# Output and down projections of a decoder trunk: two column chunks together, seven products on sums in place of eight for 42 channel pairs

## The chip, the cores and the metric

The kernel runs on one core of a Trainium2 chip. The metric is the device time of one execution in microseconds (us). Engines are named as the profile names them: PE is the matrix engine (PEld its weight loads), DVE the vector engine, ACT the scalar engine, POOL the GpSimd engine, SP the engine that issues most DMAs. An instruction queue is worked off in order on each engine; engines wait for one another by semaphores.

## The reference

A hidden state of 256 tokens by 2048 channels passes through one Mamba-2 layer with a gated feed-forward network (FFN) and one attention layer with a second FFN; after each of the four parts comes `x <- LayerNorm(alpha * x + f(x))`. What matters here are three matrix products:

```python
y @ w_out                                # 256 x 4096 by 4096 x 2048, end of the Mamba mixer
(jax.nn.silu(gate) * val) @ w_down       # 256 x 5632 by 5632 x 2048, end of either FFN
h = layer_norm(DEEPNORM_ALPHA * h + mix, ln_mix_g[layer], ln_mix_b[layer])
```

All is float32. The kernel splits each float32 operand into a high part, rounded to the type that PE multiplies fast, and a low part (the rest), and computes high*high + high*low + low*high: three matmuls for one product.

## The kernel before, in words

**Weights.** The matrices lie in DRAM cut into tiles of 128 x 1024 float32 (512 KB), in the order of use. One tile is one *step*. `load()` (L165) fetches a tile into one of four `raw` buffers, with a DMA on SP's queue. `split()` (L175) makes the high part `hi` on ACT (a cast, L191) and the low part `lo` on DVE (a subtraction, L192), in a ring of four buffers each, and then issues the next load. `splits(i)` (L196) is called once in step i and lets the splits run at most three steps ahead of the products.

**Output and down projections (mode "X").** The 2048 output columns are four chunks of 512. A chunk is the sum over all channels: `w_out` has 32 channel tiles of 128, `w_down` 44. A step holds two channel tiles (a *channel pair*) of one chunk. `half(i, t)` (L204) makes the products of 128 tokens (t is 0 or 1) with the step's two 128 x 512 weight blocks: six matmuls, so twelve in a step. The activations are stationary: `yT` (after the Mamba mixer) or `gT` (in an FFN) hold high and low parts with channels on partitions. Chunk after chunk is finished; the last four steps of the fourth chunk (eight at the kernel's end) are its *tail*, whose second token half comes at the very end in two pieces of 256 columns. The other big products (mode "W") put the weights in the stationary place.

**PSUM.** Eight banks of 128 x 512: three pairs `acc` and two single tiles `tp`.

**Norm.** `class Norm` (L373 on) adds each finished chunk to alpha times the residual (`add2`, `begin`, `add`), gathers statistics, and normalises; `chain` (L863 on) hangs these onto steps: `at(i, f)` runs f after the products of step i, `amid` in their middle, `beyond` after one half. `turn` transposes the result into `hT`, the input of the next products.

**Where the activations come from.** Mamba: for each of eight groups of 512 channels (16 steps and some small products each) `z_split(g)` (L817) writes the high and low part of 512 channels into `yT`, 12 steps into the following group. FFN: `gated(j, half)` (L974) does so for 256 channels into `gT`. During the three projections `hT` (128 x 16 channel tiles x high and low x 256 tokens) is not read, apart from serving as extra split buffers in the last steps.

**Order.** There is no scheduler: each engine gets its instructions in the order in which the Python code runs.

## Time and profile before

| | |
|---|---|
| median of three runs | 2517.62 us (2517.26 to 2519.15) |
| profiled execution, its own time | 2518.55 us |
| its span, first to last instruction | 2516.6 us |
| PE busy in the span | 2502.3 us (99%) |
| DVE, ACT, POOL busy | 1664.1, 1366.1, 75.8 us |
| bytes moved by DMA | 503 MB, 200 GB/s |
| mean granted TensorE clock | 0.999 |

The three projections lie at about 490 to 670 us (Mamba), 1155 to 1395 us (first FFN) and 2263 to 2506 us (second FFN) of the span. Times below are microseconds from the span's start. A busy matmul in the profile lasts longer than its share of the stream, since matmuls overlap: what one costs is read from how many start in a stretch.

### The profile page before, as it was taken

What the parts mean: (1) busy time and instruction counts of PE and PEld (TensorE: products, weight loads), DVE (VectorE), ACT (ScalarE), POOL (GpSimd) and SP (SyncE); (2) the same over time, 40 slices, a digit from 0 to 9 for tenths busy, and PEclk for the clock granted to TensorE, in tenths of its full rate; (3) what the DMA queues carried; (4) which work ended last, traced back from release to release, by engine and by line L of the source; (5) the groups of instructions that cost most, each with busy time, mean ns of one, the idle gap of its engine ahead of it and who ended that gap; (6) DMA issues with size and microseconds to landing.
All of it is one profiled execution on the core that took longest, in us unless ns stands there. A gap on an engine that the chain in (4) does not pass through costs nothing.

```text
span 2516.6 us, 35530 instructions
## 1 busy us (share of the span) xinstructions
PE 2502.3 (99%) x13711; PEld 2159.3 (86%) x13711; DVE 1664.1 (66%) x2134; ACT 1366.1 (54%) x1779; POOL 75.8 (3%) x96
## 2 busy tenths in 40 slices
PE   9999999999999999999999999999999999999998
PEld 8888888888888888888888888888888888888887
DVE  7878778855766767675445656655776776775545
ACT  6677787643465555554334445543555555554333
POOL 0000000000200000000000200000200000000001
PEclk9999999999999999999999999999999999999999
DMA  7665665666666565656676665457666566566575
GB/s 265 201 191 193 216 200 181 205 206 221 212 210 197 188 195 189 197 186 197 202 237 208 212 193 169 160 173 236 211 200 196 189 195 190 193 193 202 197 226 167
DMA packets 142264, 503.07 MB, mean 200 GB/s; under 512 B 15872, under 2 KB 16384, under 8 KB 142096
## 3 DMA queue, kind: packets, MB, share of 16 engines
q1 hardware_dynamic: 136976, 483.45, 58.9%
q0 software_dynamic: 4832, 16.85, 2.2%
q8 instruction: 107, 1.75, 0.3%
q14 instruction: 61, 0.50, 0.1%
q10 hardware_dynamic: 288, 0.52, 0.1%
HBM read 492.30 MB, written 8.45 MB: 199 GB/s over the span
## 4 chain that ended last, share of the span: by engine, by line
PE 96%; DVE 2%; DMA 1%; ACT 1%; issue 1%; SPq 0%; DVEq 0%; ACTq 0%
PE acc L252 40%; PE acc L254 20%; PE acc L222 11%; PE acc L217 11%; PE acc L218 11%; DVE lo L192 1%; DMA raw<-in_w 1%; PE acc L756 1%; ACT hi L191 0%; PE tp L765 0%; PE acc L739 0%; PE tp L1029 0%; DVE r L431 0%; PE tp L1063 0%; PE tp L217 0%
## 5 line engine op out<-in xcount | busy, mean ns | idle before, releaser
L192 DVE TENSOR_TENSOR lo<-raw,hi 128x1024 fp32r<-128x1024 f32 (+1 forms) x871 | 1064.4, 1226 | 709.4 <-ACT hi L191 704.9
L191 ACT CAST hi<-raw 128x1024 fp32r<-128x1024 f32 (+1 forms) x871 | 912.6, 1050 | 870.5 <-PE acc L222 396.0
L252 PE MATMUL acc<-hT,hi 128*128 128x512 f32 x4496 | 1083.8, 392 | 0.5 <-ACT hi L191 0.5
L252 PEld LDWEIGHTS acc<-hT,hi 128*128 128x128 f32 x4496 | 822.3, 188 | 160.0 <-ACT hi L191 1.0
L254 PEld LDWEIGHTS acc<-hT,lo 128*128 128x128 f32 x4496 | 556.1, 188 | 24.7 <-DVE lo L192 1.3
L254 PE MATMUL acc<-hT,lo 128*128 128x256 f32 x4496 | 563.3, 277 | 0.9 <-DVE lo L192 0.9
L218 PE MATMUL acc<-lo,gT 128*128 128x512 f32 x668 | 259.6, 389 | 0.0
L217 PE MATMUL acc<-hi,gT 128*128 128x512 f32 x668 | 259.6, 389 | 0.0
L222 PE MATMUL acc<-hi,gT 128*128 128x512 f32 x668 | 205.5, 389 | 0.0
L218 PEld LDWEIGHTS acc<-lo,gT 128*128 128x128 f32 x668 | 125.4, 188 | 26.0
L217 PEld LDWEIGHTS acc<-hi,gT 128*128 128x128 f32 x668 | 125.4, 188 | 25.9
L222 PEld LDWEIGHTS acc<-hi,gT 128*128 128x128 f32 x668 | 125.3, 188 | 26.0
L217 PE MATMUL acc<-hi,yT 128*128 128x512 f32 x244 | 95.0, 389 | 0.0
L218 PE MATMUL acc<-lo,yT 128*128 128x512 f32 x244 | 94.7, 388 | 0.0
L217 PE MATMUL acc<-hi,hT 128*128 128x512 f32 x192 | 78.8, 410 | 0.0
L566 DVE TENSOR_TENSOR u<-u,acc 128x512 f32<-128x512 f32 x108 | 73.5, 682 | 7.9 <-ACT u L565 7.9
L593 DVE SCALAR_TENSOR_TENSOR g<-u,cols,g 128x254 f32<-128x254 f32 (+1 forms) x176 | 73.5, 478 | 4.8 <-ACT g L588 4.8
L218 PE MATMUL acc<-lo,hT 128*128 128x512 f32 x192 | 75.4, 393 | 0.0
L222 PE MATMUL acc<-hi,yT 128*128 128x512 f32 x244 | 74.9, 388 | 0.0
L979 ACT CAST gT<-v 128x512 fp32r<-128x512 f32 x44 | 27.3, 621 | 84.6 <-DVE v L978 84.6
L593 DVE SCALAR_TENSOR_TENSOR v<-u,cols,v 128x254 f32<-128x254 f32 (+1 forms) x176 | 73.1, 477 | 0.0
L424 POOL TENSOR_TENSOR rs<-rs,mhalf 128x1 f32<-128x1 f32 x8 | 7.4, 930 | 1981.1 <-DVE nb L425 1981.1
(234 smaller groups left out, 1809.7 us busy)
## 6 DMA issues: line engine op xcount, KB each, us to landing
raw<-in_w SPq DMA_DIRECT2D x881, 512.0 KB, 4.0
mA<-acum_d POOLq DMA_DIRECT2D x16, 512.0 KB, 6.9
hres<-r POOLq DMA_DIRECT2D x12, 512.0 KB, 6.3
r<-hres SPq DMA_DIRECT2D x12, 512.0 KB, 5.0
eA<-acum_d POOLq DMA_DIRECT2D x16, 128.0 KB, 8.6
r<-in_x SPq DMA_DIRECT2D x4, 512.0 KB, 5.2
gb<-in_ln_mix_g SPq DMA_DIRECT2D x8, 256.0 KB, 5.4
gb<-in_ln_mix_b SPq DMA_DIRECT2D x8, 256.0 KB, 5.5
```

What stands on the lines that cost most here:

```text
L191: nc.scalar.copy(h[:, sl], t[:, sl])
L192: nc.vector.tensor_sub(l[:, sl], t[:, sl], h[:, sl].bitcast(F32))
L217: nc.tensor.matmul(a, th, h[:, kk, sl], start=k == first, stop=False)
L218: nc.tensor.matmul(a, th, l[:, kk, sl], start=False, stop=False)
L222: nc.tensor.matmul(a, ch.x.lo(k)[:, ts], h[:, kk, sl], start=False, stop=k == last)
L252: nc.tensor.matmul(banks[j], h[:, (kk * nj + j) * P:(kk * nj + j + 1) * P], ch.x.both(k), start=begins, stop=ends, skip_group_check=True)
L254: nc.tensor.matmul(banks[j][:, :S], l[:, a, n * P:(n + 1) * P], ch.x.hi(k), start=begins, stop=ends, skip_group_check=True)
L424: nc.gpsimd.tensor_tensor(self.rs[:, h, :], self.rs[:, h, :], mhalf[:, 0, :], op=OP.pow)
L566: nc.vector.tensor_add(dst, dst, p[:, :, :S])
L593: nc.vector.scalar_tensor_tensor(d, u[:, i % 2, :S - k], c1(self.at_w, w[n - 1 - k] + self.ia + i), d, op0=OP.mult, op1=OP.add)
L756: nc.tensor.matmul(ps[64 * q:64 * q + 64, c, j * P:(j + 1) * P], G[g]["xdt"][:, c, h * 64:(h + 1) * 64], G[g]["A", c][:, h, :], start=True ...
L979: nc.scalar.copy(h, v[:, sl])
```

## The change

Two chunks of columns, a and b, are now worked together (`Duo`), in two duos for each projection. In a step the letters mean: `a` or `b`, a plain step as before (one channel pair, one chunk, twelve matmuls); `A` and `B`, two steps that share one channel pair. A *sum pair* has four activation blocks (two channel tiles by two token halves) and four weight blocks (two channel tiles by two chunks), so eight block products. They are replaced by seven, of sums of activation blocks with sums of weight blocks: `A` makes two of them, `B` five, three matmuls each, 21 in place of 24. The seven results go to eight PSUM banks, all there are. 4 and 6 channel pairs of the two duos of `w_out` and 8 and 8 of each `w_down` are sum pairs, 42 in all; the other pairs stay plain. The order of steps is set by `duo()`: some plain steps, then mostly `A B a b` repeated, then the rest of the plain ones.

- The sums of weights are made by `split_sums` on DVE (y = ra + rb's second block, z = y + a block of ra, and y's next), with high and low parts, in two tiles that were free then (`mA` or `gb`). A's raw tile is kept until B is split, and two loads are issued together after that.
- The ring of `hi` and `lo` has five buffers in place of four.
- The sums of activations are made earlier, 22 times, by `make_sums`, called from `z_split` (six times) and `gated(j, 0)` (eight times for each FFN). They are written to DRAM from SP's queue (512 KB each) and fetched into `hT` from POOL's queue at the beginning of the projection (`fetch_sums`).
- The results are put together by `Norm.sums`, nine DVE operations of 512 columns after the last sum pair of each duo.
- The residual is fetched at the beginning of a duo, and `add2` of the third chunk comes with the first `b` step after the last `a` step (for `w_out` that is the beginning of the tail).

The core of the diff:

```diff
+RING = LA + 2
+SUMS = {DI: (4, 6), DFF: (8, 8)}
+KEEP = 3
...
-    out += some("X", "mamba_w_out", 0, 0, 4, DI // P) + ffn(0)
+    out += duos("mamba_w_out", 0, DI // P, TAIL) + ffn(0)
...
+def duo(nk, which, tail):
+
+    sums = [2 * m for m in range(SUMS[nk * P][which])]
+    rest = [p for p in range(nk // 2) if p not in sums]
+    a, b, keep = list(rest), list(rest), max(tail, TAIL)
+    lead = "aaa" if which else "abababab" if nk == DI // P else "abababa"
+    items = [(n, {"a": a, "b": b}[n].pop(0)) for n in lead]
+    for p in sums:
+        items += [("A", p), ("B", p)]
+        if len(a) > KEEP:
+            items.append(("a", a.pop(0)))
+        if len(b) > keep:
+            items.append(("b", b.pop(0)))
+    return items + [("a", p) for p in a] + [("b", p) for p in b]
...
+    def split_sums(i):
+
+        ra, rb = raw_t.pop(i - 1), raw_t.pop(i)
+        (yh, yl), (zh, zl) = (ring_tiles() for _ in range(2))
...
+        nc.scalar.copy(wh, rb[:, 0])
+        yf, zf = (steps[i][0].tmp() for _ in range(2))
+        nc.vector.tensor_add(yf, ra, rb[:, 1:2, :].to_broadcast([P, 2, NC]))
+        nc.vector.tensor_sub(wl, rb[:, 0], wh.bitcast(F32))
+        nc.scalar.copy(yh, yf)
+        nc.vector.tensor_add(zf[:, 0], yf[:, 0], ra[:, 1])
+        nc.vector.tensor_add(zf[:, 1], zf[:, 0], rb[:, 0])
+        nc.vector.tensor_sub(yl, yf, yh.bitcast(F32))
+        nc.scalar.copy(zh, zf)
+        nc.vector.tensor_sub(zl, zf, zh.bitcast(F32))
+        hi_t[i], lo_t[i] = [wh, yh, zh], [wl, yl, zl]
+        load()
+        load()
...
+    def one(i, b, unit, h, l):
...
+        nc.tensor.matmul(a, xh, h, start=begins, stop=False)
+        nc.tensor.matmul(a, xh, l, start=False, stop=False)
+        nc.tensor.matmul(a, xl, h, start=False, stop=ends)
...
+        if name == "A":
+            one(i, "P1", (0, 0), h[:, 0], l[:, 0])
+            one(i, "p3", 3, h[:, 1], l[:, 1])
...
+        if name == "B":
+            (wh, yh, zh), (wl, yl, zl) = h, l
+            one(i, "P2", (1, 0), wh, wl)
+            one(i, "p5", 0, yh[:, 0], yl[:, 0])
+            one(i, "P7", 2, yh[:, 1], yl[:, 1])
+            run(mid, i)
+            one(i, "p6", 1, zh[:, 0], zl[:, 0])
+            one(i, "p4", (1, 1), zh[:, 1], zl[:, 1])
...
+    def make_sums(m, tile, v):
+
+        hi, lo = (tile.rearrange("p (a q t) -> p a q t", a=2, q=4)[:, a] for a in range(2))
+        (a11, a21), (a12, a22) = ([v[:, k, h * P:(h + 1) * P] for h in range(2)] for k in range(2))
+        nc.vector.tensor_sub(lo[:, 0], a21, a22)
+        nc.vector.tensor_sub(lo[:, 2], a11, a21)
+        nc.vector.tensor_sub(lo[:, 1], a11, lo[:, 0])
+        nc.vector.tensor_sub(lo[:, 3], a12, lo[:, 1])
+        nc.scalar.copy(hi.bitcast(F32R), lo)
+        nc.vector.tensor_sub(lo.bitcast(F32R), lo, hi)
+        nc.sync.dma_start(sums_d[m], tile)
+
+    def fetch_sums(m):
+        nc.gpsimd.dma_start(hT[:, 2 * m:2 * m + 2].rearrange("p k a t -> p (k a t)"), sums_d[m])
...
+            before(du.first - 2 + m // 3, fetch_sums, m)
...
+                at(du.sum_at[-1] + n, norm.sums, d, n)
...
+        if g < max(SUMS[DI]):
+            make_sums(g, mp.tile([P, 2 * NC], F32, tag="st", name="st", bufs=1), y[:, :2])
```

Where the change moves instructions: three places on DVE, the order before and now. L192 of before is L315 now, L821 is L1076, L723 is L973, L566 is L816, L416 and L419 (the third chunk's addition and statistics) are L631 and L658, L411 is L631.

First, DVE in the Mamba stage where the group's `z_split` stands (`mA` is the masked decay, `sz` the gate, `lo` a weight tile's low part). Before:

```order
L192 TENSOR_TENSOR lo<-raw,hi 128x2x512
L821 TENSOR_TENSOR yT<-y,yT 128x4x256
L723 TENSOR_TENSOR mA<-mA,cb 128x1024
L566 TENSOR_TENSOR sz<-sz,acc 128x512
L192 TENSOR_TENSOR lo<-raw,hi 128x2x512
```

Now, for six of the eight groups (`st` holds the sums of activations):

```order
L1076 TENSOR_TENSOR yT_160<-y_3929,yT_160 128x4x256
L570 TENSOR_TENSOR st_4374<-y_3929 128x128
L571 TENSOR_TENSOR st_4374<-y_3929 128x128
L572 TENSOR_TENSOR st_4374<-y_3929,st_4374 128x128
L573 TENSOR_TENSOR st_4374<-y_3929,st_4374 128x128
L575 TENSOR_TENSOR st_4374<-st_4374 128x512
L973 TENSOR_TENSOR mA_4099<-mA_4099,cb_4231 128x1024
L816 TENSOR_TENSOR sz_4383<-sz_4383,acc_4233 128x512
L315 TENSOR_TENSOR lo_4393<-raw_4270,hi_4392 128x2x512
```

Five operations stand between the low part of `yT` and the next mask; the last of them needs a cast of ACT that needs the four before it.

Second, DVE in the middle of the output projection. Before, one subtraction for each step and the addition of a finished chunk:

```order
L192 TENSOR_TENSOR lo<-raw,hi 128x1024 x16
L416 SCALAR_TENSOR_TENSOR r_5411<-r_5411,acc 128x512 x2
L419 BN_STATS bnst<-r_5411 128x6 x4
```

Now, for one `A B a b` (`mA` is y or z, `u` the low part of B's first block; the three subtractions of the last row are those of a, b and the next A):

```order
L284 TENSOR_TENSOR mA<-raw 128x1024
L285 TENSOR_TENSOR u<-raw,u 128x512
L287 TENSOR_TENSOR mA<-mA,raw 128x512
L288 TENSOR_TENSOR mA<-mA,raw 128x512
L289 TENSOR_TENSOR lo<-mA,hi 128x1024
L291 TENSOR_TENSOR lo<-mA,hi 128x1024
L315 TENSOR_TENSOR lo<-raw,hi 128x1024 x3
```

For the same four steps DVE has nine operations in place of four.

Third, DVE at the end of the output projection. Before:

```order
L192 TENSOR_TENSOR hT<-raw,hT 128x1024 x3
L192 TENSOR_TENSOR lo<-raw,hi 128x1024 x3
L411 SCALAR_TENSOR_TENSOR r_5997<-r_5997,acc 128x512
L401 SCALAR_TENSOR_TENSOR r_5997<-r_5997,acc 128x512
```

Now (`r2` is the residual of the third chunk, `r3` of the fourth):

```order
L315 TENSOR_TENSOR lo_6249<-raw_6201,hi_6248 128x1024
L631 TENSOR_TENSOR r2_5730<-r2_5730,acc_5656 128x512 x2
L658 BN_STATS bnst_4984<-r2_5730 128x6 x4
L315 TENSOR_TENSOR lo_6275<-raw_6223,hi_6274 128x1024
L315 TENSOR_TENSOR lo_6281<-raw_6227,hi_6280 128x1024
L631 TENSOR_TENSOR r3_5767<-r3_5767,acc_5732 128x512
L315 TENSOR_TENSOR lo_6294<-raw_6246,hi_6293 128x1024
L631 TENSOR_TENSOR r3_5767<-r3_5767,acc_5733 128x512
```

The third chunk's addition and statistics had 16 subtractions between them and the fourth chunk's first addition, and now have two; one more subtraction comes before the fourth chunk's second addition.

## Rows read from the trace of the kernel before

**Rows 1.** The page: the span, and busy time and share of each engine with its number of instructions.

```profile
span 2516.6 us, 35530 instructions
PE 2502.3 (99%) x13711; PEld 2159.3 (86%) x13711; DVE 1664.1 (66%) x2134; ACT 1366.1 (54%) x1779; POOL 75.8 (3%) x96
```

**Rows 2.** Who PE waited for over the whole run, the longest: us in total, times, longest.

```profile
PE tp L538 <- POOL ident masks.py:199: 1.4, 1, 1.4
PE acc L254 <- DVE lo L192: 0.9, 1, 0.9
```

**Rows 3.** Busy time of each engine (and its instructions) in stretches inside the three projections, then TensorE clock, busy share of the DMA engines and GB/s; the fourth stretch lies behind the end of the output projection, the last is the end of the span.

```profile
core 0: us, PE busy (x) PEld busy (x) DVE busy (x) ACT busy (x) POOL busy (x), PEclk, DMA share, GB/s
520.00:640.00 120.00, 120.00 (x531) 99.41 (x530) 65.65 (x71) 48.23 (x47) 0.00 (x0) 1.00 0.66 219
1200.00:1380.00 180.00, 180.00 (x795) 149.03 (x795) 89.91 (x86) 71.58 (x69) 0.00 (x0) 1.00 0.65 211
2300.00:2480.00 180.00, 180.00 (x796) 149.07 (x794) 88.66 (x85) 70.69 (x68) 0.00 (x0) 1.00 0.65 214
684.00:688.00 4.00, 3.78 (x20) 2.63 (x19) 4.00 (x6) 2.12 (x3) 0.53 (x1) 1.00 1.02 359
2510.00:2517.00 7.00, 0.00 (x0) 0.00 (x0) 2.35 (x5) 0.00 (x0) 2.27 (x2) 0.61 0.43 150
```

**Rows 4.** DVE in order of time, four places where its operations follow one another: start, us, line, tile, number of operations.

```profile
418.81 0.41 DVE L690 TENSOR_TENSOR cb<-tp,tri 128x256 f32<-128x256 f32 x1
419.14 1.22 DVE L192 TENSOR_TENSOR lo<-raw,hi 128x1024 fp32r<-128x1024 f32 x1
...
450.29 0.69 DVE L768 TENSOR_TENSOR eA<-eA,tp 128x512 f32<-128x512 f32 x1 [1.27 <-PE tp L765]
451.01 0.69 DVE L769 TENSOR_TENSOR y<-y,eA 128x512 f32<-128x512 f32 x1
...
478.42 0.42 DVE L809 SCALAR_TENSOR_TENSOR sz<-sz 128x256 f32<-128x256 f32 x1
478.88 0.42 DVE L810 SCALAR_TENSOR_TENSOR sz<-sz 128x256 f32<-128x256 f32 x1
...
680.15 2.30 DVE L192 TENSOR_TENSOR lo<-raw,hi 128x1024 fp32r<-128x1024 f32 x1
```

**Rows 5.** DVE in order of time around the sixth group's `z_split` (L821).

```profile
435.32 1.22 DVE L821 TENSOR_TENSOR yT<-y,yT 128x1024 fp32r<-128x1024 f32 x1
436.45 1.22 DVE L723 TENSOR_TENSOR mA<-mA,cb 128x1024 f32<-128x1024 f32 x1
437.59 0.68 DVE L566 TENSOR_TENSOR sz<-sz,acc 128x512 f32<-128x512 f32 x1
438.19 1.22 DVE L192 TENSOR_TENSOR lo<-raw,hi 128x1024 fp32r<-128x1024 f32 x1
439.32 1.28 DVE L741 TENSOR_TENSOR xdt<-acc,aux 128x512 f32<-128x512 f32 x2
440.52 0.68 DVE L742 TENSOR_TENSOR xe<-xdt,aux 128x512 f32<-128x512 f32 x1
441.12 3.49 DVE L192 TENSOR_TENSOR lo<-raw,hi 128x1024 fp32r<-128x1024 f32 x3
```

**Rows 6.** ACT's copy to `sz` there in order of time, the page's rows of ACT casts of 1024 and of 512 columns (count, then busy us and mean ns of one, then idle before), and PE in order of time there (L254 has the low parts of two steps, eight matmuls each).

```profile
434.12 0.58 ACT L565 COPY sz<-acc 128x512 f32<-128x512 f32 x1
...
L191 ACT CAST hi<-raw 128x1024 fp32r<-128x1024 f32 (+1 forms) x871 | 912.6, 1050 | 870.5 <-PE acc L222 396.0
L979 ACT CAST gT<-v 128x512 fp32r<-128x512 f32 x44 | 27.3, 621 | 84.6 <-DVE v L978 84.6
...
442.81 1.99 PE L254 MATMUL acc<-hT,lo 128*128 128x256 f32 x16
```

**Rows 7.** The first FFN, DVE behind `gated(j, 0)` and PE, in order of time.

```profile
1035.39 0.69 DVE L980 TENSOR_TENSOR gT<-v,gT 128x512 fp32r<-128x512 f32 x1 [0.69 <-ACT gT L979]
1036.54 1.23 DVE L192 TENSOR_TENSOR lo<-raw,hi 128x1024 fp32r<-128x1024 f32 x1 [0.45 <-ACT hi L191]
...
1042.49 1.99 PE L254 MATMUL acc<-hT,lo 128*128 128x256 f32 x16
```

**Rows 8.** Weight loads from issue to landing: the median between 520 and 640 us, and shortest, median and longest of the whole run.

```profile
raw<-in_w SPq DMA_DIRECT2D x44, 512.0 KB, 4.2
...
DMA to landing us min/median/max: 3.0/4.0/9.7
```

**Rows 9.** The beginning of the output projection: PE's first matmul and the addition on DVE that empties the last PSUM bank of the Mamba stage.

```profile
489.89 0.39 PE L217 MATMUL acc<-hi,yT 128*128 128x512 f32 x1
...
493.42 0.68 DVE L566 TENSOR_TENSOR sz<-sz,acc 128x512 f32<-128x512 f32 x1
```

**Rows 10.** The end of the output projection: DVE from the last two subtractions to the scaling of the first chunk, and the transposes (L357) on PE.

```profile
657.88 1.22 DVE L192 TENSOR_TENSOR lo<-raw,hi 128x1024 fp32r<-128x1024 f32 x1 [1.26 <-ACT hi L191]
659.95 1.23 DVE L192 TENSOR_TENSOR lo<-raw,hi 128x1024 fp32r<-128x1024 f32 x1 [0.84 <-ACT hi L191]
662.21 0.69 DVE L401 SCALAR_TENSOR_TENSOR r<-r,acc 128x512 f32<-128x512 f32 x1 [0.44 <-PE acc L222]
665.47 0.78 DVE L436 SCALAR_TENSOR_TENSOR r<-r,rs,gb 128x512 f32<-128x512 f32 x1 [0.47 <-POOL rs L424]
...
666.32 0.63 PE L357 MATMUL tp<-ident,r 128*128 128x128 f32 x4
```

More of the change, by code (lines that the diff above doesn't have):

```diff
@@ L193, in split, with in_ring @@
         hi_t[i], lo_t[i] = h, l
-        load()
+        if kind(i) != "A":
+            load()
+    def in_ring():
+        return sum(2 if kind(k) == "B" else 1 for k in hi_t if k not in spare)
     def splits(i, most=2):
@@ L200, in splits @@
             ahead = LA + 1 + sum(i <= k < j for k in spare)
-            if j < min(i + ahead, n_steps) and (j in spare or sum(k not in spare for k in hi_t) < LA + 1):
+            if j < min(i + ahead, n_steps) and (j in spare or in_ring() + (2 if kind(j) == "B" else 1) <= RING):
                 split()
@@ L208, in half @@
         sl = slice(0, NC) if piece is None else slice(piece * HC, (piece + 1) * HC)
-        a = ch.part[t] if piece is None else ch.piece[piece]
         ts = slice(t * P, (t + 1) * P)
-        cut_k = ch.nk - 2 * ch.tail
-        first = 0 if piece is None else cut_k
-        last = (cut_k if t and piece is None else ch.nk) - 1
-        for kk in range(2):
-            k = 2 * s + kk
+        if ch.mode == "D":
+            name, p = ch.items[s]
+            ks, side = (2 * p, 2 * p + 1), ch.sides[name]
+            if piece is None:
+                a, begins, ends = ch.into({"a": ("P2", "p4"), "b": ("p3", "N22")}[name][t], i)
+            else:
+                a, begins, ends = side.piece[piece], i == side.at[-side.tail], i == side.last
+        else:
+            ks, side = (2 * s, 2 * s + 1), ch
+            a = ch.part[t] if piece is None else ch.piece[piece]
+            cut_k = ch.nk - 2 * ch.tail
+            begins = ks[0] == (0 if piece is None else cut_k)
+            ends = ks[1] == (cut_k if t and piece is None else ch.nk) - 1
@@ L216, in half @@
+        for kk, k in enumerate(ks):
             th = ch.x.hi(k)[:, ts]
-            nc.tensor.matmul(a, th, h[:, kk, sl], start=k == first, stop=False)
+            nc.tensor.matmul(a, th, h[:, kk, sl], start=begins and kk == 0, stop=False)
             nc.tensor.matmul(a, th, l[:, kk, sl], start=False, stop=False)
         run(inner, (i, t, piece))
-        for kk in range(2):
-            k = 2 * s + kk
-            nc.tensor.matmul(a, ch.x.lo(k)[:, ts], h[:, kk, sl], start=False, stop=k == last)
+        for kk, k in enumerate(ks):
+            nc.tensor.matmul(a, ch.x.lo(k)[:, ts], h[:, kk, sl], start=False, stop=ends and kk == 1)
@@ new lines, in duo_products @@
+    def duo_products(i):
+        ch, s = steps[i]
+        ch.use(i)
+        name, p = ch.items[s]
+        h, l = hi_t[i], lo_t[i]
+        if name == "A":
+            one(i, "P1", (0, 0), h[:, 0], l[:, 0])
+            one(i, "p3", 3, h[:, 1], l[:, 1])
+            run(mid, i)
+            done(i)
+            return splits(i)
+        if name == "B":
[3 more added lines that the diff above has]
+            one(i, "P7", 2, yh[:, 1], yl[:, 1])
+            run(mid, i)
+            one(i, "p6", 1, zh[:, 0], zl[:, 0])
+            one(i, "p4", (1, 1), zh[:, 1], zl[:, 1])
+            done(i)
+            return splits(i)
+        side = ch.sides[name]
+        ends = side.tail and i >= side.at[-side.tail]
+        if side.tail and i == side.at[-side.tail]:
+            side.piece = [tp_tile()[:, :HC] if q or side.tail == LAST else acc_pair()[:, 0, :HC] for q in range(2)]
+        half(i, 0)
+        if ends:
+            if i < side.last:
+                return splits(i)
+            for q in range(2):
+                for j in side.at[-side.tail:]:
+                    half(j, 1, q)
+                    if q:
+                        done(j)
+            return
+        run(mid, i)
+        splits(i)
+        half(i, 1)
+        done(i)
@@ L980, in gated @@
             nc.vector.tensor_sub(lo, v[:, sl], h.bitcast(F32))
+            if half == 0 and j < max(SUMS[DFF]):
+                make_sums(j, t4k("st").rearrange("p a n -> p (a n)"), v[:, :2])
         for j, (cg, cv) in enumerate(up):
@@ L1096, in yoco_kernel @@
         spare[end - 3 + e] = 4 * e
-    at(down1[3].first + 6, n3.gb_psum, 0)
+    at(end - LAST + 1, n3.gb_psum, 0)
     at(end - LAST + 2, n3.gb_psum, 2)
@@ L1152 @@
         m = m if layer is None else m[layer]
+        if mode == "D":
+            for kind, p in duo(nk, *both):
+                tiles.append(_np.stack([m[k * P:(k + 1) * P, c:c + NC] for k, c in blocks(kind, p, c0)], axis=1))
+            continue
         for c, n, k, per in cut(mode, nk, both):
```

172 lines of the change are left out of this document (146 added, 26 removed).

## The prediction

> **What bounds the kernel now.** I read the page first: PE is busy 2502.3 of 2516.6 us, no other engine more than 66% [rows 1]. Then who PE waited for: no entry above 1.4 us, weights 0.9 us in all [rows 2]. Of the 14.3 us without PE, 7 or more lie behind its last matmul [rows 3]. So the time is the number of matmuls times their distance, and whatever feeds PE is hidden, with reserves that differ from place to place. [...]
>
> **The products.** 531, 795 and 796 matmuls start in 120, 180 and 180 us [rows 3]: 0.226 us each. Each of 42 channel pairs loses 24 - 21 = 3, together 126 x 0.226 = 28.5 us, all on the path. Everything below asks what of it is given back.
>
> **DVE inside the projections.** Operations of 1024 columns follow one another every 1.14 us (435.32, 436.45, 437.59), those of 512 every 0.60 (437.59 to 438.19) [rows 5], and one that needs the result of the one just before 0.72 (450.29 to 451.01) [rows 4]. Four steps needed 4 x 1.14 = 4.6 us of DVE beside 48 matmuls = 10.85 us. An `A B a b` needs six operations of 1024 (6.84) and three of 512 (0.60 + 0.60 + 0.72): 8.8 us beside 45 matmuls = 10.2 us. That is 86%, so PE still sets the pace, by 1.4 us a group. An addition with one operand repeated stands in no row. Its nearest row is the 1.14 above; the slowest subtraction of 1024 columns took 2.30 [rows 4], but at 680 us, beside POOL's elementwise work, and POOL computes nothing in the projections (busy 0.00 in them) [rows 3]. I take 1.14. With 2.30 for all six a group would take 15.7 us of DVE; that end goes into the last rival.
>
> **Weight loads.** A's and B's raw tiles come free together only when y and z are made, and two loads go out at once. That closes a loop: load L, cast of the next A on ACT (1.05 [rows 6] and some 0.05 to start), its subtraction (1.14), then y and z (1.14 + 0.60 + 0.60 + 0.72), less 0.66 because A's tile is free before the last addition: L + 4.7 us for one group. With the median landing of 4.2 us [rows 8] it is 8.9 us, under 10.2, so it is hidden. With L = 5.5 it equals PE's 10.2. Shortest and longest landing in the run are 3.0 and 9.7 [rows 8]. [...]
>
> **Making sums of activations, Mamba.** Here DVE has little reserve. Behind `z_split` it gets four subtractions of 128 columns and one of 512 that waits for ACT. A line through the distances 1.14, 0.60 and 0.33 (418.81 to 419.14) [rows 4, 5] gives 0.20 for 128 columns, and 0.33 where it needs the one before (0.46 instead of 0.33 for 256 columns, 478.42 to 478.88). From 436.45 the four end at 437.46; ACT, free from 434.12, casts 512 columns in 0.62 [rows 6], to 438.1; the last subtraction holds DVE until 438.74. Everything behind is 2.3 us later: the first of the three subtractions from 441.12 ends at 442.34 + 2.3 = 444.64. PE uses that low part in the second half of the sixteen matmuls from 442.81, at 443.72 [rows 6]. So PE waits 0.9 us where it had 1.4 us in hand. The other low parts have 3 us and more, and DVE catches up before the next group, so this comes once in each of six groups: 5.6 us. It is bounded by 0 (should DVE start this stretch earlier thanks to the fifth ring buffer) and 6 x 2.3 = 13.8 us.
>
> [...]
>
> **Making sums, FFN.** The same 2.3 us behind the low part at 1035.39 move the subtraction at 1036.54 to 1038.8; PE reads it in the block from 1042.49 [rows 7]. Nothing is lost. If that cover were gone, each of 16 calls could cost what a Mamba call does.
>
> **SP's queue.** Each store of sums waits on SP for DVE, with weight loads behind it. These loads wait for subtractions that stand behind the sums on DVE anyway, so SP adds nothing.
>
> **Fetching sums.** Six or eight fetches of 512 KB begin with each projection, beside weight loads that run the DMA engines at 65% and 211 to 219 GB/s; full, they moved 359 GB/s [rows 3]. The spare 140 GB/s moves 4 MB in 30 us. The first sums are needed after seven or eight steps of 12 x 0.226 = 2.7 us, 19 us and more, and one further pair every 10 us. If loads got only half of 359, a tile took 2.9 us to move instead of the 2.7 that PE needs: 1.7 us behind after eight steps. Bounds 0 and 1.7 for each projection; I take 0.5, since loads of up to 9.7 us cost PE almost nothing before [rows 2, 8]: 1.5 us in all.
>
> **Beginning and end of the output projection.** The second step now wants the bank that is emptied at 493.42 + 0.68 = 494.1; PE reaches the half that uses it at 489.89 + 18 x 0.226 = 493.96: 0.2 us waited [rows 9]. In the FFNs the bank's copy is not queued behind so much, 0. At the end, the third chunk's two additions and four statistics of 256 columns (2 x 0.60 + 4 x 0.33 = 2.5 us) and one more subtraction (1.14) come among operations that had 1.26, 0.84 and 0.44 us of idle time ahead of them [rows 10]. DVE is 3.6 - 2.5 = 1.1 us late at the addition of 662.21, hence at the scaling that the transposes of 666.32 need (665.47 + 0.78 = 666.25) [rows 10]: 1.0 us on PE. The FFNs have more steps between. Putting the seven results together takes nine operations, 6 us over three steps that leave 3 x (2.7 - 1.14) = 4.7; the rest runs into the next step, whose low parts are made three steps ahead.
>
> **The sum**, against the profiled execution's own 2518.55 us: -28.5 + 5.6 + 1.5 + 0.2 + 1.0 = -20.2, 2498.35 us. That execution stood 0.93 us above the median of the runs, so 2497.4 us.
>
> **Rivals.**
> - *The Mamba stage absorbs its share.* The fifth ring buffer lets ACT cast earlier, or DVE's backlog begins earlier. For it: DVE waited for ACT's casts in many places. Against it: in rows 5 DVE is busy without a gap, and order is fixed. All but about 1 us of the losses goes: 2490 us.
> - *The loop of loads sets the pace in part.* L at 5.7 us makes 10.4 a group, 0.2 x 42 = 8 us more: 2505 us. For it: two loads at once, the fetches beside them. Against: 4.2 us at 65% DMA.
> - *Slower: the same loop takes everything.* From L = 6.15 us on, an `A B a b` takes the 10.85 us of before, the 28.5 us are gone and the 8.3 us of losses stay: 2526 us. The place is the raw tiles of A and B; it decides from 6.15 us. DVE at 2 us for some of its six long operations (10.85 - 8.8 = 2.1 us more in a group) would do the same. For it: loads of up to 9.7 us. Against: that is over twice the median's excess over the shortest, in every group.
> - *The fetches stall the beginnings,* by the 1.7 us bound or somewhat more each time: 2502 us.
>
> **How the numbers follow.** Forecast 0.58, its own range 2493 to 2502; the first rival 0.17, the partial loop 0.12, the fetches 0.06, slower 0.07. The range 2488 to 2508 leaves out the slower case and the worse parts of the loop and fetches. A measurement of this kernel tells 0.2%, 5 us, from no change. Faster by that means below 2512.6: forecast, first rival, fetches and most of the loop, 0.89; within it 0.05 (a loop near break-even); slower 0.06.
>
> **What would show it.** 126 matmuls fewer, at 0.226 us. PE's waits: six of about 0.9 us on L315's low parts in the Mamba stage, at the first `lo` behind `xe`. In the projections DVE busy at 80 to 90% with gaps in each group and PE without; ACT waiting for raw tiles in the casts of A would be the loop's mark, PE waiting for L289 or L291 its price. Wrong would be: PE waits in every group, or waits for `hT` at the first A.

## The result and the profile after

The changed kernel takes 2504.69 us (median of four executions, 2503.27 to 2506.38) against 2517.57 us before: a ratio of 0.9948, 95% interval 0.9931 to 0.9965. It is faster by about 13 us. The forecast was 2497.4 us with a range of 2488 to 2508: the direction and the range hold, the middle is 7 us off. The profiled execution took 2503.27 us.

The page, as in [rows 1], and who PE waited for, as in [rows 2] (us in total, times, longest):

```profile
span 2501.6 us, 35870 instructions
PE 2477.3 (99%) x13585; PEld 2139.5 (86%) x13585; DVE 1898.3 (76%) x2509; ACT 1425.7 (57%) x1885; POOL 87.6 (4%) x118
```

```profile
PE tp L551 <- DVE r L675: 7.0, 3, 4.0
PE acc L447 <- DVE lo L315: 3.3, 6, 0.8
PE acc L352 <- DVE sz L816: 1.7, 1, 1.7
```

PE has 126 matmuls fewer, as reckoned, and three kinds of waits that it did not have. Where they lie is seen when the span is cut at the first matmul of each stage: stretch, its length, PE's busy time and matmuls, granted clock, DMA share, GB/s. The six stages are Mamba, output projection, first FFN up to its down projection, that projection, attention with the second FFN, last projection.

```profile
1.43:493.18 491.75, 488.31 (x3021) 1.00 0.65 215
493.18:672.35 179.17, 173.47 (x810) 0.99 0.67 228
672.35:1159.10 486.75, 486.60 (x2821) 1.00 0.60 206
1159.10:1392.83 233.73, 230.97 (x1038) 0.99 0.66 229
1392.83:2261.99 869.16, 868.40 (x4846) 1.00 0.59 200
2261.99:2491.22 229.23, 229.23 (x1057) 1.00 0.65 225
```

```profile
1.43:489.89 488.46, 487.08 (x3021) 1.00 0.64 207
489.89:668.23 178.34, 178.34 (x839) 1.00 0.65 218
668.23:1155.62 487.39, 487.09 (x2823) 1.00 0.60 195
1155.62:1395.75 240.13, 240.13 (x1085) 1.00 0.64 210
1395.75:2266.25 870.50, 869.54 (x4846) 1.00 0.59 194
2266.25:2506.12 239.87, 239.87 (x1104) 1.00 0.62 202
```

The second fence is the kernel before, cut in the same way. The differences of the lengths are +3.3, +0.8, -0.6, -6.4, -1.3 and -10.6 us, with -0.1 behind the last matmul: the 15.0 us by which the span is shorter. Products alone would give -6.8, -10.9 and -10.9 in the three projections (30, 48 and 48 matmuls of 0.2267, as 45 start in the 10.2 us of a group). The last projection has nearly its whole gain. The output projection gave all of its gain back and 0.8 more, the first down projection 4.5.

**The Mamba stage** shows the mechanism that was predicted. DVE behind the low part of `yT` in the third group, then PE at the low parts, in the first group and in the third (start, us, engine and line, operation, shape, count, idle time before and what ended it):

```profile
289.38 0.28 DVE L570 TENSOR_TENSOR st<-y 128x128 f32<-128x128 f32 x1
289.58 0.28 DVE L571 TENSOR_TENSOR st<-y 128x128 f32<-128x128 f32 x1
...
291.08 0.69 DVE L575 TENSOR_TENSOR st<-st 128x512 fp32r<-128x512 f32 x1 [0.69 <-ACT st L574]
291.69 1.22 DVE L973 TENSOR_TENSOR mA<-mA,cb 128x1024 f32<-128x1024 f32 x1
...
296.35 3.49 DVE L315 TENSOR_TENSOR lo<-raw,hi 128x1024 fp32r<-128x1024 f32 x3
```

```profile
198.26 1.22 PE L447 MATMUL acc<-hT,lo 128*128 128x256 f32 x8 [0.51 <-DVE lo L315]
...
296.04 1.08 PE L447 MATMUL acc<-hT,lo 128*128 128x256 f32 x8
297.63 1.22 PE L447 MATMUL acc<-hT,lo 128*128 128x256 f32 x8 [0.51 <-DVE lo L315]
```

The five operations hold DVE from 289.38 to 291.69, 2.31 us (predicted 2.3), and PE stands in the middle of the first `lo` behind `xe`, once in each of six groups. From one subtraction of `yT` to the next (L821 before, L1076 now) a group takes 49.7 us in place of 48.9; from the first to the seventh these are 298.31 and 293.40 us, so the six groups cost 4.9 us. The stage is only 3.3 us longer because the first of these subtractions comes 1.9 us sooner (188.87 in place of 190.81): two waits of 0.45 and 0.91 us ahead of it, at 12 and 105 us of the profile before, are not in this one.

**Inside the projections** DVE has a gap in every `A B a b` and PE none. One group of the first down projection, from its first operation (L284) to the first behind it, and the stretch around it, in the form of [rows 3]:

```profile
1243.18 1.22 DVE L284 TENSOR_TENSOR gb<-raw 128x1024 f32<-128x1024 f32 x1
...
1250.87 2.59 DVE L315 TENSOR_TENSOR lo<-raw,hi 128x1024 fp32r<-128x1024 f32 x2 [0.98 <-ACT hi L314]
1253.38 0.68 DVE L641 SCALAR_TENSOR_TENSOR r<-r,acc 128x512 f32<-128x512 f32 x1
```

```profile
1190.00:1350.00 160.00, 160.00 (x708) 132.53 (x707) 142.05 (x153) 85.44 (x90) 0.00 (x0) 1.00 0.61 210
```

DVE is busy 142 of 160 us, 89%, and PE 160 of 160.

**At the end of the output projection** PE has nothing to do from about 664.9 on. DVE there (its counterpart is [rows 10]), and then PE's next instruction, with its like at the end of the first down projection:

```profile
661.21 1.23 DVE L315 TENSOR_TENSOR lo<-raw,hi 128x1024 fp32r<-128x1024 f32 x1 [0.76 <-ACT hi L314]
662.35 0.68 DVE L631 TENSOR_TENSOR r<-r,acc 128x512 f32<-128x512 f32 x1
663.79 1.23 DVE L315 TENSOR_TENSOR lo<-raw,hi 128x1024 fp32r<-128x1024 f32 x1 [0.77 <-ACT hi L314]
664.94 0.68 DVE L631 TENSOR_TENSOR r<-r,acc 128x512 f32<-128x512 f32 x1
...
668.18 0.78 DVE L675 SCALAR_TENSOR_TENSOR r<-r,rs,gb 128x512 f32<-128x512 f32 x1 [0.46 <-POOL rs L663]
```

```profile
669.01 0.97 PE L551 MATMUL tp<-ident,r 128*128 128x128 f32 x4 [4.05 <-DVE r L675]
...
1389.37 1.10 PE L551 MATMUL tp<-ident,r 128*128 128x128 f32 x4 [2.75 <-DVE r L675]
```

In the kernel before, the second addition (L401) started at 662.21, right when PE had finished the products for it; now it starts 4.4 us after that point (PE is 1.5 us earlier here, 660.5). Two subtractions stand ahead of it, weights of the next stage, and both waited for casts; ACT itself stood 1.72 and 1.53 us for the loads of these tiles. Then comes a cost that no term of the sum had. The engines' busy times, clock, DMA share and GB/s behind the two long waits, in the form of [rows 3]:

```profile
669.20:672.60 3.40, 3.40 (x17) 3.40 (x17) 1.23 (x4) 0.66 (x2) 2.54 (x2) 0.50 0.00 0
1389.40:1392.80 3.40, 3.40 (x16) 3.40 (x17) 1.36 (x3) 0.81 (x2) 2.55 (x2) 0.50 0.00 0
```

The granted clock is 0.50 for 3.4 us at each place, and there products of 256 columns start 0.21 us apart (671.07, 671.28, 671.49), where the kernel before has 0.12 (667.51, 667.63, 667.75). From the first of these transposes to the first product of the next stage PE takes 3.34 and 3.46 us (669.01 to 672.35, 1389.37 to 1392.83), and in the kernel before 1.91 and 1.90 (666.32 to 668.23, 1393.85 to 1395.75): another 1.43 and 1.56 us lost. The first down projection bears this out: 2.75 + 1.56 are 4.3 of the 4.5 us that it gave back. Before the change the clock stood at 1.00 through the ends of all three projections (650 to 672, 1390 to 1400 and 2500 to 2506 us).

### The profile page after: what moved, and what is told of

The parts are those of the page before. It is cut to its first block, busy times and chain, and to the rows that moved or that the text cites. A ratio compares the mean times of both kernels' runs of the same rounds, so it can differ in the third digit from the quotient of the medians.

```text
span 2501.6 us, 35870 instructions
## 1 busy us (share of the span) xinstructions
PE 2477.3 (99%) x13585; PEld 2139.5 (86%) x13585; DVE 1898.3 (76%) x2509; ACT 1425.7 (57%) x1885; POOL 87.6 (4%) x118
## 4 chain that ended last, share of the span: by engine, by line
PE 92%; DVE 5%; DMA 1%; ACT 1%; issue 1%; POOL 0%; SPq 0%; DVEq 0%; ACTq 0%
PE acc L445 38%; PE acc L447 19%; PE acc L352 8%; PE acc L353 8%; PE acc L356 8%; PE acc L375 2%; PE acc L374 2%; PE acc L376 2%; DMA raw<-in_w 1%; DVE lo L315 1%; PE tp L375 1%; PE tp L374 1%; PE tp L376 1%; DVE mA L973 1%; DVE y L1070 0%
## 5 line engine op out<-in xcount | busy, mean ns | idle before, releaser
L315 DVE TENSOR_TENSOR lo<-raw,hi 128x1024 fp32r<-128x1024 f32 (+1 forms) x829 | 1007.4, 1225 | 299.4 <-ACT hi L314 289.3
L314 ACT CAST hi<-raw 128x1024 fp32r<-128x1024 f32 (+1 forms) x829 | 861.7, 1049 | 366.5 <-issue 112.0
L447 PEld LDWEIGHTS acc<-hT,lo 128*128 128x128 f32 x4496 | 556.4, 188 | 27.8 <-DVE lo L315 4.5
L447 PE MATMUL acc<-hT,lo 128*128 128x256 f32 x4496 | 564.5, 277 | 3.3 <-DVE lo L315 3.3
L353 PE MATMUL acc<-lo,gT 128*128 128x512 f32 (+1 forms) x412 | 160.0, 388 | 0.0
L352 PE MATMUL acc<-hi,gT 128*128 128x512 f32 (+1 forms) x412 | 160.0, 388 | 0.0
L816 DVE TENSOR_TENSOR u<-u,acc 128x512 f32<-128x512 f32 x108 | 74.0, 685 | 95.6 <-ACT u L815 95.5
L815 ACT COPY u<-acc 128x512 f32<-128x512 f32 x108 | 63.0, 584 | 145.4 <-PE acc L445 145.2
L356 PE MATMUL acc<-hi,gT 128*128 128x512 f32 (+1 forms) x412 | 126.5, 388 | 0.0
L352 PEld LDWEIGHTS acc<-hi,gT 128*128 128x128 f32 x412 | 77.3, 188 | 16.1
L353 PEld LDWEIGHTS acc<-lo,gT 128*128 128x128 f32 x412 | 77.3, 188 | 15.9
L356 PEld LDWEIGHTS acc<-hi,gT 128*128 128x128 f32 x412 | 77.3, 188 | 15.9
L286 ACT CAST hi<-gb 128x1024 fp32r<-128x1024 f32 x32 | 33.7, 1054 | 65.3 <-DVE gb L284 65.3
L352 PE MATMUL acc<-hi,yT 128*128 128x512 f32 (+1 forms) x164 | 63.8, 389 | 1.7 <-DVE sz L816 1.7
L353 PE MATMUL acc<-lo,yT 128*128 128x512 f32 (+1 forms) x164 | 63.6, 388 | 0.0
```

The lines of the kernel that those rows point to most:

```text
L314: nc.scalar.copy(h[:, sl], t[:, sl])
L315: nc.vector.tensor_sub(l[:, sl], t[:, sl], h[:, sl].bitcast(F32))
L352: nc.tensor.matmul(a, th, h[:, kk, sl], start=begins and kk == 0, stop=False)
L353: nc.tensor.matmul(a, th, l[:, kk, sl], start=False, stop=False)
L356: nc.tensor.matmul(a, ch.x.lo(k)[:, ts], h[:, kk, sl], start=False, stop=ends and kk == 1)
L447: nc.tensor.matmul(banks[j][:, :S], l[:, a, n * P:(n + 1) * P], ch.x.hi(k), start=begins, stop=ends, skip_group_check=True)
```

## Experiments

Twelve kernels, all variants of the changed one. Differences of 2 to 4 us lie inside the intervals of their ratios (about 0.0015 either way, 4 us), so that verdicts on one wait rest on that wait in the trace, and the times only support them. The waits, which are read from one profiled execution of each kernel, vary too. The wait at the end of the output projection, first in three kernels whose edits leave the ends alone (e3, e4, e10), then in e1, e2 and e11:

```profile
669.27 1.12 PE L551 MATMUL tp<-ident,r 128*128 128x128 f32 x4 [4.27 <-DVE r L675]
668.85 1.12 PE L551 MATMUL tp<-ident,r 128*128 128x128 f32 x4 [5.10 <-DVE r L681]
666.55 1.11 PE L551 MATMUL tp<-ident,r 128*128 128x128 f32 x4 [3.56 <-DVE r L678]
...
667.57 0.75 PE L551 MATMUL tp<-ident,r 128*128 128x128 f32 x4 [2.80 <-DVE r L678]
668.91 0.66 PE L551 MATMUL tp<-ident,r 128*128 128x128 f32 x4 [1.85 <-DVE r L675]
668.41 0.66 PE L551 MATMUL tp<-ident,r 128*128 128x128 f32 x4 [2.78 <-DVE r L675]
```

With ends as in the changed kernel (itself, e3, e4, e8 and e10) this wait is 3.56 to 5.10 us, and the one at the first down projection 2.60 to 3.32. What lies below these ranges is an effect of the edit; its size is known to a microsecond or so and no better.

**e1: gamma and beta.** The change moved their fetches (L614, `fetch_gb`; 256 KB each) from the beginning of the third chunk to the three steps behind the last sum pair. I had overlooked it. e1 leaves out two of the three at each of the two ends; its second and third chunk use the first chunk's.

```diff
+            if self.duos and self.g is not lfg[1] and c in (1, 2):
+                self.gb[c] = self.gb[0]
+                return
```

> This kernel leaves out the fetches of gamma and beta for the second and third chunk at the end of the output projection and of the first down projection; those chunks use the first chunk's (that part of the result is another one). Of 1.5 MB that the changed kernel moves there in the last 20 us, 0.5 MB are left. Theory T1 (the fetches, which the change moved from the third chunk's beginning to the steps after the last sum pair, take bandwidth from the weight loads of the last steps; the casts and subtractions of these loads stand on DVE ahead of the fourth chunk's additions): loads land in about 4.5 us in place of up to 7.5, PE's waits at the two ends fall from 4.05 and 2.75 us to about 1 and 0.5, the clock stays at 1.00, and the time falls by 6 to 9 us. Theory T2 (the fifth ring buffer lets one more subtraction stand between the two additions): each wait falls by less than 1 us, the time by less than 3. Theory T3 (the nine operations that put the seven results together hold DVE up): the waits stay, the time falls by less than 1 us.

2501.37 us, ratio 0.9935 (0.992 to 0.995). The waits at the two ends fell from 4.05 and 2.75 to 2.80 and 2.34 us, and the clock still fell at both (its mean over the run is 0.997, as in the changed kernel). T1 holds for some 1.25 and 0.41 us, far less than I expected; the second is hardly more than the waits vary.

**e2: the fifth ring buffer.** Outside the duos the ring has four buffers again.

```diff
-            if j < min(i + ahead, n_steps) and (j in spare or in_ring() + (2 if kind(j) == "B" else 1) <= RING):
+            if j < min(i + ahead, n_steps) and (j in spare or in_ring() + (2 if kind(j) == "B" else 1) <= (RING if kind(j) in "abAB" else RING - 1)):
```

> Ring of five for steps of the duos alone, four for all others: at the three chunk ends with a tail of four the fourth subtraction of the following stage no longer stands between the two additions of the fourth chunk, as before the change. T2 (the order is the cause): the waits of 4.05 and 2.75 us fall to 1 us or less, the time by 6 us or more. T1 (late loads): the additions come some 2 us earlier, since the fourth subtraction waited for a late load, but the third one is late as well, so that about 2 us of the first wait and 1 us of the second remain; the time falls by 3 to 5 us, more if the clock no longer falls. T3: the waits fall by the 1.1 us of the one subtraction at most.

2501.46 us, 0.9933 (0.9918 to 0.9948). Waits of 1.85 and 1.56 us are left, and the clock fell behind the first alone (0.50 from 669.7 to 673 us). This is what T1 foretold for it: the subtraction between the additions goes, the late one ahead of them stays.

**e3 and e4: the beginning, and the Mamba stage.**

```diff
-            before(du.first - 2 + m // 3, fetch_sums, m)
+            before(du.first + 1 + m, fetch_sums, m)
```

> The sums of activations are fetched one in each step from the second step of a projection on, in place of three in each step from two steps ahead of it. If the wait of 1.66 us at the beginning of the output projection comes from the weight load that took 8.75 us beside 3 MB of fetches (ACT's cast of it stands ahead of the copy that empties the bank), the load takes 5 us or less, the wait falls to 0.3 us or less and the time by 1.5 to 2 us. If it comes from the bank that the first b step wants, as the prediction had it, or from the order on ACT, the wait stays above 1 us.

2504.67 us, and 1.3 us of the wait stayed, but the edit tested nothing: POOL's queue was empty, and it issued the fetches from 484 us on as before. Moving a DMA in the code did not move it in time here.

```diff
+        if then is None:
+            return split_made(m, tile)
+        at(then, split_made, m, tile)
```

> In the Mamba stage the second part of making sums (cast, subtraction of 512 columns, store) comes three steps later; the four small subtractions stay. If PE's six waits of 0.5 to 0.76 us come from DVE held up by 2.3 us of which the last subtraction and its wait for ACT are 1.3, no wait on L447 is left, each of six groups gets 0.7 to 0.8 us shorter, and the time falls by 4 to 5 us. If four small operations alone are too much at this place, about half of the waits is left and the time falls by 2 us; if the later place is as full, the wait turns up there and the time stays.

2501.40 us, 0.9937 (0.9922 to 0.9951). Three of the six waits are gone, 1.9 of 3.3 us remain: the middle case. Four small operations still hold DVE for 0.93 us. (Its profiled execution was the slowest of the four, 2504.84 us, with a wait of 1.41 us at 10 us and the wait of 5.10 us above; neither place was edited.)

**e7: both ends repaired.** Gamma and beta are fetched earlier and into activations that are used up, and the third chunk's addition comes two steps later; e2's line is in it too. The core of the rest:

```diff
+                t = bufs[t][:, 4 * c:4 * c + 2].rearrange("p k a t -> p (k a t)").rearrange("p (i n) -> p i n", i=2)
...
-                amid(chs[c].end, norm.add2, c) if c < 2 else beyond(chs[2].end, 0, None, norm.add2, c)
+                amid(chs[c].end, norm.add2, c) if c < 2 else beyond(chs[2].end + (2 if nxt and norm.duos else 0), 0, None, norm.add2, c)
```

> Three edits at the ends of the output projection and of the first down projection together: ring of four outside the duos (as in e2), gamma and beta of the first three chunks fetched in the middle of the second duo into activations that are used up there (from POOL's queue), and the addition of the third chunk two steps later. T1 and T2 are each a part: e1 took 1.25 and 0.41 us from the waits of 4.05 and 2.75, e2 2.20 and 1.19. A further cause, T4: at the end of the first down projection DVE stood 3.13 us at the third chunk's addition, waiting for PE, with the subtractions and so the release of raw tiles behind it. If these three are all, the waits at both ends fall below 0.5 us, the clock stays at 1.00 there, and the time is 8 to 10 us below the changed kernel's (2495 to 2497). If a wait of 1 us or more is left, something else holds the additions, and the subtraction just before them tells what it waited for.

2499.75 us, 0.9932 (0.9915 to 0.9949), above the 2495 to 2497 that I expected. The end of the first down projection is free of waits, and that stage takes 229.25 us in place of 233.73. At the end of the output projection two are left (line, what it waited for, us, times, longest):

```profile
PE tp L551 <- DVE r L679: 1.9, 1, 1.9
PE acc L352 <- DVE r L635: 1.8, 1, 1.8
```

The second is my own doing: the tail's last products want the bank that the third chunk's addition, now two steps later, empties. The clock fell at neither end (mean over the run 0.999, as before the change).

**e8, e9, e10: fetches that really come later.** POOL first adds a column of a weight tile to itself, and so waits for that tile's load.

```diff
+    pace = base.tile([P, 8], F32, name="pace")
...
+            v = raw_t[pos["split"]][:, 0, :1]
+            nc.gpsimd.tensor_tensor(pace[:, m:m + 1], v, v, op=OP.add)
...
-            before(du.first - 2 + m // 3, fetch_sums, m)
+            before(du.first + 1 + 2 * m, fetch_sums, m)
```

> In e3 the fetches were only written later; POOL, which had nothing to do, issued them at the same time as before (from 484 us on), so that nothing was tested. Here POOL waits ahead of each fetch but the first for a weight load of the step (it adds one column of the raw tile to itself): one fetch of 512 KB in two steps from the beginning of each projection. If the six fetches make the load late that took 8.75 us, it lands within 5.5 us, the wait of 1.66 us (1.17 to 1.66 in the runs so far) falls to 0.3 us or less, and the time by 1 to 2 us. If the bank or ACT's order were the cause, the wait stays above 1 us. Should the sums come too late for the first sum pair, PE waits at L374 instead.

> e7 and e8 together, and the making of sums in the Mamba stage in two parts, the second five steps later (e4 had three; there three of six waits were left). If the causes add up, PE's waits after the beginning of the run are below 3 us in all, and the time is 2489 to 2494 us: 8 to 10 us for the ends, 1.5 for the start, 2 to 4 for the Mamba stage. If they hide one another (a wait taken away turns up at the next place) the time stays above 2496 us.

2544.74 us, 1.0108 (1.0093 to 1.0123), and 2541.16 us, 1.0092 (1.0077 to 1.0107). The wait at the beginning was gone in both, but stages without any edit were slower. The new tile is 32 bytes in each partition. e10 puts the column into spare columns of a tile that was there:

```diff
-            nc.gpsimd.tensor_tensor(pace[:, m:m + 1], v, v, op=OP.add)
+            nc.gpsimd.tensor_tensor(mhalf_tile[:, 8 + m], v, v, op=OP.add)
```

> e8 again, with the column that POOL writes in spare columns of a tile that was there, in place of a new tile of 32 bytes in each partition, which moved all tiles behind it by 32 bytes. e8 was 40 us slower with fewer waits: between 900 and 1000 us 566 matmuls started in place of 585. If the place of the tiles is the cause, 584 to 586 start there again and the time is 2502 to 2504 us; the wait at the beginning of the output projection is 0.3 us or less, as in e8, against 1.66 in the changed kernel. If POOL's waiting or the later fetches slow PE, it stays near 2540 us.

2502.86 us, 0.9941 (0.9927 to 0.9954). A stretch of the first FFN, where nothing was edited, in e8 and then in e10, in the form of [rows 3]:

```profile
900.00:1000.00 100.00, 100.00 (x566) 87.01 (x565) 70.09 (x98) 53.82 (x70) 0.00 (x0) 1.00 0.61 200
```

```profile
900.00:1000.00 100.00, 100.00 (x584) 88.13 (x583) 73.05 (x104) 55.83 (x74) 0.00 (x0) 1.00 0.61 203
```

e10 differs from e8 in nothing but that tile and has the old rate again (585 in the changed kernel), so the place of the tiles is the cause; what about the place costs time, no run shows. The fetches are confirmed too: the weight load issued at 487.3 us, from issue to landing (shortest, median, longest of one), first in the changed kernel, then in e10:

```profile
DMA to landing us min/median/max: 8.8/8.8/8.8
```

```profile
DMA to landing us min/median/max: 4.2/4.2/4.2
```

In the changed kernel ACT's cast of this tile came at 496.12, its copy to `sz` at 497.08 behind it in order, DVE's addition, which empties the bank, at 498.35 behind the same tile's subtraction (497.20), and PE at 499.08 after 1.66 us. In the nine kernels with the early fetches this wait is 0.99 to 1.66 us; in the four with paced fetches (e8, e9, e10, e12) PE does not wait there.

**e11: the output projection's sum pairs divided otherwise.**

```diff
-SUMS = {DI: (4, 6), DFF: (8, 8)}
+SUMS = {DI: (5, 5), DFF: (8, 8)}
```

> Five and five sum pairs in the two duos of the output projection in place of four and six, the same number in all; nothing else. Behind the last pair then stand nine plain steps and not seven (as in the first down projection), and the last two groups are A B a b where they were A B b. Theory T3' (at the end of the output projection DVE comes out of the last groups and the nine assembling operations late, so it frees raw tiles late and in a bunch; e7 had four loads issued within 3.6 us that took 5.7 us each): the wait of 4.05 us falls to 2.75 or less, as at the end of the first down projection, and with one making of sums less in the Mamba stage (0.8 us) the time falls by 2 to 4 us. If the gamma and beta fetches and the fifth ring buffer are all there is, the wait stays at 3.5 to 4 us and the time falls by 1 us.

2501.48 us, 0.9937 (0.9923 to 0.9950). The wait of 4.05 fell to 2.78 us. What of this is due to the longer way from the last pair to the end is not shown, since two more things moved: the gamma and beta fetches, which hang on the last pair, were issued by 645.84 in place of 654.54 us, and DVE now stands 3.13 us at the third chunk's addition (650.48), as at the first down projection. The clock stayed at 1.00 behind this wait, though it had fallen behind one of 1.85 in e2: how long PE waits does not decide it alone.

**e5 and e6: DVE's reserve.** The last subtraction of a sum pair is done twice (e5) or three times (e6).

> The last subtraction of each of the 42 sum pairs is done twice: 1.14 us more of DVE for each A B a b, where e6 had 2.28 more, 0.9 us of wait in each group and 61 us in all. If the reserve in a group is 1.4 us, as predicted, PE waits for no low part inside the groups (no 0.9 us waits every 11.4 us) and the three projections take what they take in the changed kernel, but for the ends, where DVE is late already: 2503 to 2512 us. If the reserve is used up (DVE at 100% by other work), about half of e6's loss, 30 us, is seen.

> The last subtraction of each of the 42 sum pairs is done three times: 2.28 us more of DVE for each A B a b. The prediction put DVE at 8.8 us of PE's 10.2 for such a group, a reserve of 1.4 us. If that is right, DVE becomes the bound by 0.9 us in each of the 32 or so groups that have both plain steps, and the time is 20 to 40 us above the changed kernel's, with PE waiting for lo in the groups. If DVE's operations overlap more than I reckoned, or the few plain steps at the ends of a duo make up for it, the time rises by less than 10 us.

One execution each: 2516.22 and 2565.80 us. The same stretch of the first down projection, first e5, then e6, and e6's longest entry of waits:

```profile
1220.00:1280.00 60.00, 60.00 (x267) 49.69 (x266) 57.20 (x64) 30.84 (x32) 0.00 (x0) 1.00 0.65 215
```

```profile
1220.00:1280.00 60.00, 55.49 (x239) 44.30 (x239) 59.07 (x58) 30.88 (x33) 0.00 (x0) 1.00 0.56 190
PE tp L376 <- DVE lo L292: 34.4, 35, 2.2
```

With one operation more PE still never waits in this stretch. e5's loss, above the 2503 to 2512 us expected, lies at the output projection, which took 185.2 us in place of 179.2, and at the ends; in the output projection PE waited three times for a low part of y or z (1.09, 0.88 and 0.47 us), which I had not expected. With two more a group takes 11.41 us in place of 10.2: 35 waits of some 0.9 us, with 1.2 us more for each group. That is 42 of the 61 us, which are above the 20 to 40 expected; the rest was not taken apart. A repeat was 1.26 us behind the one before and not 1.14, and DVE has no gap in these groups, so it needs 11.41 - 2 x 1.26 = 8.89 us for a group of the changed kernel (predicted 8.8).

**e12: all repairs.** e2's ring; e7's gamma and beta; its later addition in the first down projection alone; e10's fetches; e4's second part two steps later still; e11's division.

> All together: ring of four outside the duos, gamma and beta in the middle of the second duo, the third chunk's addition two steps later in the first down projection alone (in e7 it made PE wait 1.78 us for a bank at the end of the output projection), fetches paced as in e10, the second part of making sums five steps later, five and five sum pairs. If the causes are separate, PE waits less than 1 us at each end and at the start and less than 2 us in the Mamba stage, and the time is 2488 to 2493 us. If DVE at the end of the output projection is late anyway, 2 us of wait stay there and the time is 2493 to 2496 us.

2495.74 us (2492.74 to 2496.59, five executions), 0.9911 (0.9898 to 0.9925), an interval that does not touch the changed kernel's. PE's longest waits:

```profile
PE acc L447 <- DVE lo L315: 1.7, 4, 0.6
PE tp L551 <- DVE r L688: 1.6, 1, 1.6
PE tp L802 <- POOL ident masks.py:199: 1.4, 1, 1.4
```

The output projection takes 173.4 us (178.34 - 6.8 + 1.6 is 173.1) and no projection sees the clock fall before its last matmul (mean over the run 0.999). What still holds DVE for 1.6 us at its end was not settled: its third subtraction there waits 1.41 us for a cast, and that cast 1.59 us for a load. One candidate can be read from the traces. With the pairs divided 5 and 5 the pattern of the first down projection has come here, DVE standing at the third chunk's addition with subtractions behind it, and e12 moves that addition in the first down projection alone. The changed kernel there, and e12 here:

```profile
1371.46 1.28 DVE L631 TENSOR_TENSOR r<-r,acc 128x512 f32<-128x512 f32 x2 [3.13 <-PE acc L356]
...
645.65 1.28 DVE L644 TENSOR_TENSOR r<-r,acc 128x512 f32<-128x512 f32 x2 [3.13 <-PE acc L356]
```

No run moves it in the output projection with 5 and 5.

## Why the prediction was right, and where it was off

- *The products* (-28.5 us): right. 13711 - 13585 = 126, and the last projection, with no wait at its end, is 10.6 us shorter for 48.
- *DVE inside the projections, and the loop of loads*: right. 8.89 against 8.8 us, loads of 3.6 us (median of 59 between 1200 and 1350 us) against the 4.2 assumed. Of two that go out together the first, the next A, takes 3.6 as well and the second 4.7 (medians of 12 pairs); the loop's fixed part adds up to 4.6 and not 4.7, so it stands at 8.2 us, under 10.2. e5 and e6 show that the reserve in a group of a down projection is one operation and not two. Both slower rivals that lived on this fall with it. From the issue of the first to the landing of the second 5.4 us passed (median of these pairs).
- *Making sums, Mamba* (+5.6 us): right in mechanism and place, and close in size: the six groups cost 4.9 us, 0.78 for most of them against 0.93 forecast; the profile's waits of 0.50 to 0.76 are less than what was lost (the sixteen matmuls with the wait of 0.51 in their middle take 2.64 us, 296.04 to 298.68, and 1.82 in the kernel before, 442.81 to 444.63). DVE's low part comes 2.32 us later after `yT` in each group, as forecast, but PE's block of low parts also comes 0.3 us later after it (7.8 us in place of 7.5). That is so in the first of the six groups as in the last, so no earlier wait has caused it, and in e2, with four ring buffers here, it is the same; its cause is open. That the stage is 2.3 us better than forecast is in the main not this term but the two waits ahead of the first group that the profile before had. The one at 12 us comes and goes between executions (0.39 to 1.41 us in e1, e3, e4, e7 and e12, none in the changed kernel's), so this is in part luck. The small operations follow one another in 0.20 us (289.38 to 289.58), though each is busy for 0.28: the distances decide, as I took them.
- *Making sums, FFN* (0): right, no wait on L447 in either FFN.
- *Beginning of the output projection* (0.2 us for the bank) and *fetching sums* (0.5 there): each half right, the sum of them wrong. The step "loads of up to 9.7 us cost PE almost nothing" failed: the one late load stands on ACT ahead of the very copy that the bank waits for, 1.66 us. At the other two projections the fetches cost nothing (0.5 each assumed).
- *End of the output projection* (1.0 us): this is the step that failed, and with it "the FFNs have more steps between". Measured 4.05 and 2.75 us, and 1.43 and 1.56 us for the clock. I had counted DVE's operations and had not followed the loads that they wait for. Two parts are shown by an edit each: 1.5 MB of gamma and beta among the last weight loads, which I had not listed as moved (e1, clear at the first end alone), and one more subtraction let in by the fifth buffer (e2, at both). Two are argued: nine assembling operations and `A B b` groups seven steps from the end, which free raw tiles late (e11, which moves the fetches too); and, at the first down projection, DVE standing 3.13 us at the third chunk's addition with subtractions behind it (repaired together with the others in e7, not tried alone).
- *Everything else* (0): the stages between are 2.0 us shorter. No experiment touches that; the cause stays open.

Put together, in the spans: 8.8 us more than forecast at the two ends, 1.0 more at the start of the output projection, 2.3 less in the Mamba stage, 1.0 less for the other fetches, 2.0 less elsewhere; that is 4.5 of the 7.3 us that the forecast was too low. Another 2.3 lie between executions: the profiled one stood 0.9 us above the median before and 1.4 below it now. The remaining 0.5 is not accounted for. That the time lies in the range is thus in part luck: 9.8 us of cost that the sum did not have stand against 5.3 that it had too much, and without these 5.3 the time would have been 2510 us, above the range. Of the rivals, the first fell (the waits of the Mamba stage are there), and so did the one of the fetches as it was put: it had loads falling behind over eight steps, and what happened, at one beginning of three, was one late load in ACT's queue. That both come to 1.7 us is chance.

## What to carry to other kernels

When work is added to an engine with reserve, look at the ends of the stage before its middle: there the reserve is needed by what follows. Here an addition that came 4.4 us late, behind two subtractions whose casts had waited 1.72 and 1.53 us for loads, stopped PE for 4.05 us. List every DMA that an edit moves, and for each late load what stands behind its consumer on that engine. And read a wait in more than one execution before its size is trusted: with nothing edited near it, the wait at the end of the output projection lay between 3.56 and 5.10 us.

## What the runs showed of the hardware

A tile of 32 bytes in each partition, allocated ahead of the others, made the chip start 566 matmuls in 100 us where it started 584 (e8, e10), some 42 us over the kernel; the projections, whose stationary operands are the activations, were not slower (233.6 us for the first down projection in e8, 233.7 in the changed kernel). The clock fell behind waits of 1.85, 2.34 and 2.75 us (e2, e1, the changed kernel; to 0.50 for 3.3 us or more in e2 and the changed kernel) but not behind others of 1.86, 2.60 and 2.78 (e7, e8, e11). Its mean over the run was 0.997 in e1 and the changed kernel, 0.998 in e2, e8 and e11, and 0.999 in e7.
